# A list scheduler simulates the engines' timelines in its finer way: what becomes of the time?

## The chip, the cores and the metric

The kernel runs on one core of a Trainium2 chip. Its time is the device time of one execution in microseconds (us); TensorE, VectorE, ScalarE, GpSimd and SyncE (whose queue issues the DMA transfers) each run a list of instructions of their own, in order, and wait for each other by semaphores. In the profile they are PE (products), PEld (its weight loads), DVE, ACT, POOL and SP.

## The reference, cut to what matters

All in float32, 512 tokens of width 1024, two blocks of two layers each:

```python
def first_block(x, p, ...):                       # twice:
    z = rmsnorm(h) @ w_in + b_in                  # conv, pool, q, k, v, gates, index q and k
    ya = conv_module(...) * silu(c_gate)          # 31 taps, norm, product
    yb = pool_mixer(...) * silu(p_gate)
    yc = sparse_attention(q, k, v, qi, ki, wi) * silu(a_gate)   # top 128 keys of an index score
    h = h + concat([ya, yb, yc]) @ w_out
    h = h + (p[i] @ ple_w[i]) * sigmoid(h @ ple_gate_w[i])

def second_block(x, positions, meta_tokens, ...): # 16 meta tokens in front; twice:
    proj = h @ w_in[li]
    y_att = _mla(...)                             # latent attention, 4 heads
    y_rwkv, v_first = _rwkv_bidir(...)            # a recurrence, 8 heads, both directions
    h = layer_norm(a * h + concat([y_att, y_rwkv]) @ w_out[li])
    h = layer_norm(a * h + _hier_moe(h, ...))     # 32 experts, the best 2 of a token's group
```

## The kernel before, in words

The program is written with a tile framework: Python code calls one operation after another on tiles that come from pools with a fixed number of buffers, and nothing in it says when an operation runs. When the context that wraps the whole program closes, the framework's scheduler makes the list of each engine. It walks along a simulated timeline. Whenever an engine can take its next operation, it gets, of the operations that count as ready at that simulated moment (inputs done, a buffer free for the output), the one with the best priority. The priority is the order in which the Python code called them; a stretch of code can raise its own. So the simulated timeline does not appear in the result as times, only as an order: of instructions on each of the four compute engines, of transfers on SP's queue, and of who gets a buffer that comes free. On the chip each engine then runs its list strictly in order.

Stages, in the order of the program:

- `first_block` (lines 818 to 840), with `first_layer` (387 to 740) twice. Weights arrive in chunks of 256 columns (`raw`, line 291) and are split in two rounded parts, one on ScalarE (line 300), the rest on GpSimd (line 301), so that a float32 product becomes three fast ones (`mm3`, line 307). The layer's start turns normed rows (line 315) and rotates the index projections (lines 370 to 375). In the attention each unit (`terms`, lines 625 to 647, `values`, 649 to 664) makes logits (633), their maxima (636), a scaling of two columns (638), exponentials (640), a diagonal (646), turned terms (657) that VectorE or ScalarE evicts (275, 277), and values (662). Beside them the code lays six taps of the convolution (line 518, VectorE) and a share of dense projections.
- Between the blocks: norms and transposes by way of DRAM (lines 742 to 803).
- `mixers` (1258 to 1322), for each of the second block's layers: projections (1006), latent attention (1073 to 1209), and the recurrence in four pairs of heads (`rwkv_pair`, 1339 to 1726). A pair's last stage is a chain of nine steps: a product with the state (1636, added at 1638), the triangular inverse (1662, evicted at 1671), the update's product (1674, added on VectorE at 1677, two instructions a step). Its priority is raised by 300 places. Fill (projections, attention) is laid between the steps at a rate, `RATE`, that the source fixes.
- `out_rest` (1778 to 1857) and `moe` (1872 to 2086): output projection, norm, routing, then 16 pairs of experts, whose weights (100 MB a layer) stream through buffers of the pools (2227, 2231), and the norm at the end of the layer.

The lines that set priority and rate:

```python
            n += self.RATE[l]
            while fill is not None and (n > 0 or all(x == "end" for x in state)):
                ...
                c = next(fill, "end")
...
            with self.tc.high_priority(offset=self.AHEAD):      # AHEAD = 300
...
    with tile.TileContext(nc) as tc:                            # line 2328
        program(tc, A, out)
```

`lnexp2` (lines 975 to 983) makes a power of -1/2 on ScalarE by a logarithm (980) and an exponential (982).

Of the kernel before, what the change touches and what calls it, by code (L numbers as in the profile page):

```python
# [16 lines left out]
DRAM = bass.MemoryType.DRAM  # L17
# [10 lines left out]
# ---------------------------------------------------------------- constants of the shapes  # L28
def shape_constants():
    c = {}  # L30
    i = np.arange(128)
    c["ident"] = np.eye(128, dtype=np.float32)
    # lhsT of the swap x -> (-x2, x1) within each 64 rows
# [15 lines left out]
    # one over the pools' counts: of the first 16 tokens, of the later ones  # L49
# [13 lines left out]
def slot_codes():  # L63
    """per token tile and choice: the token, and its row among the choices' results"""
    v = np.zeros((128, 5, 2, 2), np.int32)
    for t, (t0, n) in enumerate(TT):
        tok = t0 + np.arange(n)
        for k in range(2):
            v[:n, t, k, 0] = tok
            v[:n, t, k, 1] = tok * 2 + k  # L70
    return v.reshape(128, 20)


def shape_constants2():
    """the second block's"""
# [9 lines left out]
    # masks of the chunk products: rows (slot, j), columns (kkd i | rd i); the b rows sit in slot q, and only they have  # L85
    # removal products there
# [10 lines left out]
    # masks of the doubling steps from blocks of 8 on, lower for T forward; the last belongs to the transposed  # L97
# [7 lines left out]
    # row j of each block of 8 on all of its partitions; a block's own columns; its unit rows, forward and backward  # L105
# [12 lines left out]
    # per choice and token tile: the token, and its row among the choices' results, less a number that no row has  # L118
# [14 lines left out]
# those of the recurrence stay only beside the mixers  # L133
# [6 lines left out]
# columns of the first block's projection  # L140
# [4 lines left out]
# per-partition parameter columns of a first-block layer  # L145
# [9 lines left out]
def cols(v):  # L155
    """[n*128] -> [128, n]"""
    return np.ascontiguousarray(v.reshape(-1, 128).T)
# [11 lines left out]
def pack_p2(x, l):  # L169
# [9 lines left out]
    for k in "gb":  # L179
        put("n1" + k, x[f"ln1_{k}_2"][l])  # L180
        # those of the norm before the layer
        put("n" + k, x[f"ln2_{k}_2"][l - 1] if l else x[f"emb_ln_{k}_2"])
# [18 lines left out]
class K:  # L201
# [26 lines left out]
    # frequently used tags  # L228
# [13 lines left out]
    def c(self, name, width=None):  # L242
        """a constant, or width columns from its first on"""
# [18 lines left out]
    # out[128, n] = in ** -0.5  # L262
# [3 lines left out]
    def load_cols(self, w, c0, n, kt=8):  # L266
        """rows (k p) of w, n columns from c0 -> [128, kt, n]"""
# [11 lines left out]
    # ------------------------------------------------------------ the first block  # L279
    # A float32 product in three passes of float32r: each operand is the sum of a rounded part and the rest, and only  # L280
    # the product of the two rests, below float32's last place, stays out.
# [6 lines left out]
    def raw(self, w, c0, n, kt):  # L288
        """kt*128 rows of w, n columns from c0"""
# [4 lines left out]
    def split_cols(self, w, c0, n):  # L294
        """n columns of w from c0 in two parts, [128, 8, n] each"""
# [8 lines left out]
    def mm3(self, ps, a, b, start, stop):  # L304
        """ps += a^T b, of their parts"""
# [3 lines left out]
    def columns(self, x, src, t):  # L309
        """a token tile's rows, turned, into its columns of x [128, 8, 512], in two parts"""  # L310
# [11 lines left out]
    def start_layer(self, l):  # L322
        """its small parameters, and its first weights"""
# [13 lines left out]
    def tile_rms(self, t, h, junk=None):  # L337
        """1/rms of a token tile's rows"""
# [7 lines left out]
    def tile_normed(self, x, t, h):  # L346
        """normed, and into its columns of x"""
# [4 lines left out]
    def zT(self, w, c, nT, m=128):  # L352
        """psum [m, 512] of columns c..c+m of the loaded chunk"""
# [5 lines left out]
    def go_on(self, topk=0):  # L359
        """what was left until the tensor engine had more to do; and some steps of the masks"""  # L360
# [17 lines left out]
    def silu_gate(self, ps, bias, hbias):  # L378
        """(tanh(z/2) + 1) * z : twice silu(z)"""
# [7 lines left out]
    def first_layer(self, l, h):  # L387
# [9 lines left out]
        # ---- index projections  # L397
# [27 lines left out]
        # ---- scores and the mask of the top 128  # L425
# [31 lines left out]
        # ---- queries, keys, values  # L457
# [25 lines left out]
        # ---- convolution: its input  # L483
# [20 lines left out]
        # ---- beside the attention: the taps, and dense work that yields its share of the tensor engine's time  # L504
# [3 lines left out]
        def conv_taps():  # L508
            # ---- the convolution
            for j in range(2):  # L510
# [3 lines left out]
                # u holds twice the gated value: the taps are halved  # L514
# [7 lines left out]
        def dense():  # L522
            # ---- the attention's gate
# [12 lines left out]
            # ---- pool mixer  # L536
# [31 lines left out]
            for j in range(2):  # L568
# [5 lines left out]
                # (psum + b) * scale, the gate to come  # L574
# [6 lines left out]
            # ---- the convolution's norm and product  # L581
# [30 lines left out]
            for j in range(2):  # L612
# [3 lines left out]
                # cs and the gate each hold twice their value: psum/2 + b, then the gate's half  # L616
# [7 lines left out]
        # ---- attention  # L624
        def terms(t, hp):
            """the softmax' terms of a tile of queries and two heads, and their sums' reciprocals"""
# [22 lines left out]
        def values(t, hp, pt, dgs):  # L649
# [3 lines left out]
            for i in range(2):  # L653
                # turned over and divided by the sum
# [29 lines left out]
        # ---- out projection and residual  # L684
# [15 lines left out]
        # ---- per-layer embedding, gated  # L700
# [39 lines left out]
    # ------------------------------------------------------------ between the blocks: the first one's result, normed, behind  # L740
    # the meta tokens; normed again: transposed and by rows, these without the gains and the biases, in DRAM
# [12 lines left out]
    def embedded(self, t, h):  # L754
        """the statistics of token tile t"""
# [21 lines left out]
        else:  # L777
            # the second norm of h*fg / r, with r*r = mean(h*h) + 1e-6: that of h*fg with r*r times its epsilon
# [30 lines left out]
    def lnexp(self, ps, scale, eps, n):  # L809
        """(ps*scale + eps) ** -0.5 of a psum tile, on the scalar engine"""  # L810
# [29 lines left out]
    # ------------------------------------------------------------ the second block  # L840
# [10 lines left out]
    def gy(self, dt=F32):  # L851
        """half of the transposed hidden state, or two of the mixers' outputs"""
        return self.g_tile("gy", [128, 2, L2], 4, dt)
# [5 lines left out]
    def wide(self):  # L859
        """1024 columns of the same store"""  # L860
# [5 lines left out]
    def rows2(self, *srcs):  # L866
        """[1024] rows of DRAM on every partition"""
# [5 lines left out]
    def stats(self, q, x, n, st, eps=1e-5):  # L873
        """the mean of x's rows, negated, and 1/deviation, of the rows' sums in st's first two columns"""
# [11 lines left out]
    def staged(tiles, *stages, between=iter(())):  # L886
        """for each tile its stages, those of later tiles before"""
# [6 lines left out]
    def scaled(self, out, q, n, g, b, fast=False):  # L894
        """out = q*g + b"""
# [7 lines left out]
    def hT_tiles(self):  # L903
        """the transposed hidden state in two parts, four [128, 2, 528] each"""
        return [(self.gy(F32R), self.big(F32R)[:, :2 * L2].rearrange("p (j t) -> p j t", j=2)) for _ in range(4)]

    def parts(self, hi, lo, x, eng=None):
        """x's rounded part, and the rest"""
# [3 lines left out]
    def angles(self):  # L912
        """cos and sin of the positions, [128 (four times 32 dims), 528], to DRAM"""
# [27 lines left out]
    def turned(self, q, t):  # L941
        """a normed token tile, transposed, in two psums"""
# [9 lines left out]
    def transposed2(self, hT, t, q):  # L952
        """those, times the gains and with the biases, in two parts"""
# [12 lines left out]
    def halves(self, lhs, rhs, m=128, start=True, stop=True, ps=None):  # L966
        """psums [m, 264] x 2 of sum_k lhs[k]^T rhs[k]"""
# [7 lines left out]
    def lnexp2(self, ps, scale, eps, out=None):  # L975
        """(ps*scale + eps) ** -0.5 of a pair of psums -> [128, 528]"""
# [12 lines left out]
    # 128 columns each of the projection: 0-1 queries, 2 keys and values, 3 the rotated keys (twice), 4-15 r, k, v, 16-18 low  # L989
    def proj_weights(self, l, i, eng=None):  # L990
        """in two parts"""
# [8 lines left out]
    def proj_tile(self, w, hT):  # L1000
        """psums [128, 264] x 2, of the parts"""
# [11 lines left out]
    def both(self, out, ps):  # L1013
        """out = the two psums"""
# [3 lines left out]
    def shifted(self, i, w, hT):  # L1018
        """the i-th tile of the recurrence's inputs; r, k and v go to DRAM"""
# [11 lines left out]
    def fill(self, l, hT, hs, yd, tiles):  # L1031
        """dense work beside the recurrence: its other inputs, the attention; yields its share of the tensor engine's time"""
# [19 lines left out]
    def rope2(self, z, o, cos, sin):  # L1052
        """o may be z"""
# [1278 lines left out]
```

## Time and profile before

| | us |
|---|---|
| median of the runs (two: 2854.81 and 2856.70) | 2855.76 |
| span of the profiled execution | 2857.8 |
| TensorE busy in it | 2472.6 |
| VectorE, ScalarE, GpSimd busy | 1496.6, 855.6, 822.8 |

The span runs from the first to the last instruction of one profiled execution, which lies 2.0 us above the median of the runs. Busy time counts overlapping instructions once. The granted clock is TensorE's, as a share of its full 2.4 GHz; its other level is 1.2 GHz. An idle time in front of an instruction is put down to what ended it.

### The profile page before, as it was taken

The numbers are of one execution on the slowest core, as the hardware profiler recorded it, in microseconds if no ns is written. First come the engines' busy times: TensorE is split into PE (matmuls) and PEld (weight loads), VectorE is DVE, ScalarE is ACT, GpSimd is POOL, SyncE is SP. The second block draws the span as 40 slices with busy tenths as digits, with TensorE's granted clock in tenths as the row PEclk, the third lists the DMA queues.
The fourth block names the chain that finished last, engine by engine and source line by source line (L and its number), as shares of the span: only waits on it lengthen the run. The fifth ranks groups of instructions, "written<-read, shape, count | busy, mean of one in ns | idle before, by whom it ended". The sixth has DMA issues, their size and how long they took to land. (4 is left out here: it accounts for less than half of the span.)

```text
span 2857.8 us, 48911 instructions
## 1 busy us (share of the span) xinstructions
PE 2472.6 (87%) x19771; PEld 1901.9 (67%) x19771; DVE 1496.6 (52%) x3308; ACT 855.6 (30%) x1698; POOL 822.8 (29%) x795
## 2 busy tenths in 40 slices
PE   7989997988996889999996889959888899969893
PEld 5766795766896777766765556549766667755552
DVE  3956234866245685566536321166866675362213
ACT  3233323233333433434402010133434344021111
POOL 5444424545421541222012100034523120120102
PEclk9999998999997989999998899979999999989997
DMA  5220122221126322101326899873220113279996
GB/s 158 60 78 30 50 82 63 63 70 38 61 64 192 108 92 85 34 29 51 124 68 217 269 369 365 280 218 118 84 89 15 44 51 120 82 261 367 371 364 234
DMA packets 312294, 394.16 MB, mean 138 GB/s; under 512 B 23683, under 2 KB 258819, under 8 KB 311809
## 3 DMA queue, kind: packets, MB, share of 16 engines
q1 hardware_dynamic: 304288, 376.70, 40.1%
q0 software_dynamic: 7776, 14.30, 1.4%
q8 instruction: 157, 2.57, 0.4%
q14 instruction: 73, 0.59, 0.1%
HBM read 352.02 MB, written 52.94 MB: 142 GB/s over the span
## 5 line engine op out<-in xcount | busy, mean ns | idle before, releaser
L301 POOL TENSOR_TENSOR wl<-raw,wh 128x1024 fp32r<-128x1024 f32 (+1 forms) x92 | 217.9, 2380 | 251.7 <-ACT wh L300 251.7
L1006 PE MATMUL sc<-gy,w 128*128 128x264 f32 x1216 | 223.9, 300 | 28.9 <-DVE ph L1864 11.3
L1006 PEld LDWEIGHTS sc<-gy,w 128*128 128x128 f32 x1216 | 183.0, 198 | 38.5 <-issue 13.3
L307 PE MATMUL ps<-wh,xh 128*128 128x256 f32 x640 | 190.6, 298 | 9.5 <-DVE a L374 9.5
L307 PE MATMUL ps<-wl,xh 128*128 128x256 f32 x640 | 184.2, 288 | 0.0
L307 PE MATMUL ps<-wh,xl 128*128 128x256 f32 x640 | 183.6, 287 | 0.0
L307 PE MATMUL ps<-xh,wh 128*128 128x512 f32 (+1 forms) x400 | 172.0, 430 | 0.0
L300 ACT ACTIVATE wh<-raw 128x1024 fp32r<-128x1024 f32 (+1 forms) x92 | 93.0, 1025 | 258.9 <-PE ps L307 154.7
L307 PE MATMUL ps<-xl,wh 128*128 128x512 f32 (+1 forms) x400 | 166.3, 416 | 0.1
L307 PE MATMUL ps<-xh,wl 128*128 128x512 f32 (+1 forms) x400 | 165.5, 414 | 0.0
L2023 POOL DMA_INDIRECT zd<-my,idx x32 | 31.6, 986 | 424.9 <-ACT my L277 424.9
L2241 PE MATMUL ps<-big,hTr 128*64 128x256 f32 x1168 | 153.9, 381 | 0.0
L1006 PE MATMUL sc<-big,w 128*128 128x264 f32 x608 | 134.1, 295 | 2.4 <-DVE big L910 2.4
L307 PEld LDWEIGHTS ps<-wh,xh 128*128 128x128 f32 x640 | 124.4, 194 | 14.0 <-DVE a L374 12.4
L307 PEld LDWEIGHTS ps<-wl,xh 128*128 128x128 f32 x640 | 124.6, 195 | 0.7
L307 PEld LDWEIGHTS ps<-wh,xl 128*128 128x128 f32 x640 | 124.6, 195 | 0.0
L2241 PEld LDWEIGHTS ps<-big,hTr 128*64 128x64 f32 x1168 | 93.1, 137 | 40.7 <-issue 2.8
L2188 DVE SCALAR_TENSOR_TENSOR mh<-mh,ps 128x256 f32<-128x256 f32 x32 | 13.5, 421 | 188.2 <-ACT mh L2187 188.2
L1006 PEld LDWEIGHTS sc<-big,w 128*128 128x128 f32 x608 | 101.1, 198 | 3.9 <-DVE big L910 3.5
L518 DVE SCALAR_TENSOR_TENSOR a<-pz,ph,a 128x512 f32<-128x512 f32 x120 | 102.0, 850 | 2.7
L1591 ACT ACTIVATE z<-ps,mix 128x512 f32<-128x512 f32 x144 | 76.8, 577 | 77.8 <-PE ps L1481 77.6
L1996 PEld LDWEIGHTS ps<-gy,big 128*128 128x128 f32 (+1 forms) x720 | 86.7, 190 | 18.8 <-issue 6.5
(500 smaller groups left out, 6037.8 us busy)
## 6 DMA issues: line engine op xcount, KB each, us to landing
big<-in_moe_w_dram SPq DMA_DIRECT2D x216, 512.0 KB, 9.2
w8m<-in_moe_w_dram SPq DMA_DIRECT2D x48, 1024.0 KB, 12.5
w<-in_moe_w_dram SPq DMA_DIRECT2D x36, 1024.0 KB, 12.3
raw<-in_w_in_dram SPq DMA_DIRECT2D x56, 512.0 KB, 3.6
big<-in_w_in_dram SPq DMA_DIRECT2D x36, 512.0 KB, 5.7
raw<-in_w_out_dram SPq DMA_DIRECT2D x16, 512.0 KB, 3.5
raw<-in_ple_gate_w_dram SPq DMA_DIRECT2D x16, 512.0 KB, 3.5
big<-zd SPq DMA_DIRECT2D x16, 512.0 KB, 8.1
```

What stands on the lines that cost most here:

```text
L300: nc.scalar.activation(hi[:, x:x + 4], v, AF.Copy)
L301: nc.gpsimd.tensor_tensor(lo[:, x:x + 4], v, hi[:, x:x + 4].bitcast(F32), op=ALU.subtract)
L307: self.nc.tensor.matmul(ps, a[x], b[y], start=start and j == 0, stop=stop and j == 2)
L518: nc.vector.scalar_tensor_tensor(acc, u[:, s:s + S], ph[:, tp + s:tp + s + 1], acc, op0=ALU.mult, op1=ALU.add)
L1006: self.nc.tensor.matmul(ps[x][:, :HALF], w[a][:, k], hT[k // 2][b][:, k % 2, x * HALF:(x + 1) * HALF], start=k == 0 and a == b == 0, stop= ...
L1591: nc.scalar.activation(Z[g][q][:, :self.WIDTH[g]], ps[:, :self.WIDTH[g]], AF.Copy, scale=self.c("half")[:, q:q + 1])
L1996: nc.tensor.matmul(ps[:, k * 128:(k + 1) * 128], h[t][:n, (4 * g + k) * 128:(4 * g + k + 1) * 128], sel[:n, t], start=t == tiles[0], stop= ...
L2023: ins = nc.gpsimd.indirect_dma_start(out=zd[:, :], out_offset=bass.IndirectOffsetOnAxis(ap=idx[:, j, 1:2], axis=0), in_=y, in_offset=None, ...
L2188: nc.vector.scalar_tensor_tensor(a, a, 1.0, p1[:, :256], op0=ALU.add, op1=ALU.mult)
L2241: nc.tensor.matmul(ps[q * 64:q * 64 + 64, :256], xT[:, k, q * 64:q * 64 + 64], w[q][k], start=k == 0, stop=k == 7)
```

## The change

The scheduler's simulated timeline comes from the framework's other, finer machine model. The program that is traced is the same: no operation, tile, pool, number of buffers, priority or rate is touched. The same diff empties comments and docstrings, leaving blank lines in their place, so line numbers stay as they are.

```diff
-    with tile.TileContext(nc) as tc:
+    with tile.TileContext(nc, schedule_with_timeline_sim=True) as tc:
         program(tc, A, out)
```

## Rows read from the trace of the kernel before

**Rows 1.** The page's first part: busy time, share of the span, instructions.

```profile
span 2857.8 us, 48911 instructions
PE 2472.6 (87%) x19771; PEld 1901.9 (67%) x19771; DVE 1496.6 (52%) x3308; ACT 855.6 (30%) x1698; POOL 822.8 (29%) x795
```

**Rows 2.** Busy time by stretches: start:end, length, engines, granted clock, DMA share, GB/s.

```profile
20.00:855.00 835.00, 761.65 (x4284) 608.72 (x4284) 462.05 (x929) 268.13 (x522) 376.39 (x281) 0.94 0.21 64
...
905.00:1555.00 650.00, 593.75 (x5853) 474.23 (x5851) 398.58 (x934) 233.63 (x472) 169.30 (x192) 0.94 0.27 88
...
1590.00:1860.00 270.00, 245.72 (x1748) 151.15 (x1744) 48.82 (x109) 29.62 (x61) 21.01 (x21) 1.00 0.97 335
...
1905.00:2530.00 625.00, 568.90 (x5747) 463.06 (x5745) 394.17 (x891) 230.55 (x455) 156.11 (x183) 0.96 0.28 90
...
2565.00:2815.00 250.00, 225.34 (x1679) 140.54 (x1677) 47.74 (x108) 29.62 (x61) 21.02 (x21) 1.00 1.05 363
```

**Rows 3.** TensorE's waits, 20 to 855: total us, times, longest.

```profile
PE po L662 <- DVE attT L275: 21.5, 10, 3.9
PE ps L315 <- DVE b L349: 14.2, 5, 5.6
PE ps L436 <- DVE a L374: 9.9, 2, 4.9
PE ps L307 <- DVE a L374: 9.5, 2, 4.8
PE px L657 <- POOL diag L646: 6.8, 6, 1.9
PE po L662 <- ACT attT L277: 6.1, 4, 2.2
```

**Rows 4.** TensorE's waits, 905 to 1555: the longest group.

```profile
PE ps L1662 <- DVE rr L1638: 5.7, 5, 1.8
```

**Rows 5.** TensorE's waits, 1905 to 2530: the longest group.

```profile
PE ps L971 <- ACT u L1708: 6.5, 3, 2.7
```

**Rows 6.** The timeline, 198 to 216: start, us, instruction, idle before and releaser.

```profile
202.66 5.14 POOL L301 TENSOR_TENSOR wl<-raw,wh 128x1024 fp32r<-128x1024 f32 x2 [2.70 <-ACT wh L300]
...
203.03 2.57 DVE L518 SCALAR_TENSOR_TENSOR a<-pz,ph,a 128x512 f32<-128x512 f32 x1
...
205.53 2.30 DVE L638 TENSOR_SCALAR sm<-sm 128x2 f32<-128x2 f32 x1
...
208.90 1.09 PE L662 MATMUL po<-attT,a 128*64 128x128 f32 x4 [3.87 <-DVE attT L275]
...
209.91 0.80 PE L307 MATMUL ps<-xl,wh 128*128 128x512 f32 x1
```

**Rows 7.** Instructions of lines 518 and 638: count, ns min/median/max.

```profile
L518 DVE SCALAR_TENSOR_TENSOR a<-pz,ph,a x120: 731/752/2896, 172.7 to 677.3; 128x512 f32<-128x512 f32 x120
L638 DVE TENSOR_SCALAR sm<-sm x32: 155/169/2397, 165.7 to 728.5; 128x2 f32<-128x2 f32 x32
```

**Rows 8.** VectorE's timeline: updates of line 1677, 1154 to 1176 and 1236 to 1249.

```profile
1163.73 0.58 DVE L1677 TENSOR_TENSOR hr<-hr,ps 64x128 f32<-64x128 f32 x2
1174.14 0.58 DVE L1677 TENSOR_TENSOR hr<-hr,ps 64x128 f32<-64x128 f32 x2
...
1240.80 0.59 DVE L1677 TENSOR_TENSOR hr<-hr,ps 64x128 f32<-64x128 f32 x2 [2.14 <-PE ps L1674]
...
1244.32 0.59 DVE L1677 TENSOR_TENSOR hr<-hr,ps 64x128 f32<-64x128 f32 x2 [0.52 <-issue]
```

**Rows 9.** Instructions of line 1677: count, ns min/median/max, first and last start.

```profile
L1677 DVE TENSOR_TENSOR hr<-hr,ps x128: 240/286/293, 1134.2 to 2489.8; 64x128 f32<-64x128 f32 x128
```

**Rows 10.** Groups by line, VectorE: count, busy us, mean ns, idle before.

```profile
L518 DVE SCALAR_TENSOR_TENSOR a<-pz,ph,a 128x512 f32<-128x512 f32 x120 | 102.0, 850 | 2.7
...
L638 DVE TENSOR_SCALAR sm<-sm 128x2 f32<-128x2 f32 x32 | 23.9, 746 | 0.4
```

**Rows 11.** Groups by line, ScalarE: the table loads.

```profile
L980 ACT ACT_TABLE_LOAD x28 | 35.9, 1283 | 0.5
...
L982 ACT ACT_TABLE_LOAD x25 | 32.1, 1283 | 0.4
```

## The prediction

> **What bounds the kernel now.** I read the page's first part first: TensorE is busy for 2472.6 us of a span of 2857.8 us, VectorE for half of it, ScalarE and GpSimd for under a third [rows 1]. So 385.2 us of the span has no product in flight, and an order of instructions can win no more than that and what the clock gives. Where it lies comes from busy time by stretches [rows 2]: in the three long stretches of dense work (the first block 20 to 855, the two layers of mixers 905 to 1555 and 1905 to 2530) TensorE is busy for 761.65, 593.75 and 568.90 us, so it is idle for 73.4 + 56.3 + 56.1 = 185.8 us. In the two expert stretches the DMA share is 0.97 and 1.05, and TensorE is idle for 24.3 + 24.7 = 49 us: there the weights' arrival sets the pace, and no order of compute changes the bytes. The remaining 385.2 - 185.8 - 49 = 150.4 us is start, routing, norms between layers and the tail: short stretches in which each operation needs the one before it.
>
> So the change can act on 185.8 us of idle time, and on the clock beside it: the granted clock was 0.94, 0.94 and 0.96 in the three stretches [rows 2], against 1.00 in the expert stretches. With levels of 1.2 and 2.4 GHz, a shortfall of 0.06 is half speed for 12% of the time, worth at most 0.06 x 835 + 0.06 x 650 + 0.04 x 625 = 114 us if TensorE had work all through it.
>
> Then I read who ended TensorE's waits. In the first block six groups make up nearly all: 34.4 us behind the attention's evictions and diagonals (21.5 + 6.1 + 6.8) and 33.6 us at the starts of the layers (14.2 + 9.9 + 9.5) [rows 3]. In the mixers the waits are scattered: the longest group of each layer is 5.7 and 6.5 us [rows 4, 5]. One of the attention's waits shows what an order can do [rows 6]: at 203.03 a convolution tap on VectorE took 2.57 us and at 205.53 a two-column scaling took 2.30 us, both while GpSimd was in its 5.14 us of weight splitting; the eviction behind them came late, and TensorE stood idle for 3.87 us before line 662, although the next thing in its queue was more products of line 307 of a group it had already begun. Those could have gone first. The list has line 662 in front, as it would if on the simulated timeline its input was there by then.
>
> **The change part by part.** No operation, tile, pool or buffer count changes; what changes is the simulated time at which an operation counts as ready, and so the order of the list that each engine gets, DMA issues on SP's queue included.
>
> *Gain in the attention.* The 34.4 us [rows 3] are waits of the kind just shown. The ends are 0 (the new list makes the same mistakes elsewhere) and 34.4. I take half, -17 us, because the example has ready work behind the wait and I have looked at one.
>
> *Gain in the mixers.* 112.4 us idle. Many small groups mean that no single dependency rules. The ends are 0 and half, 56; I take a quarter, -28 us, nearer to 0, because TensorE is already busy 91% here and much of what is left is the recurrence's own chain.
>
> *Starts of layers.* The 33.6 us [rows 3] are a norm, a transpose and a rotation in sequence. I take 0, with ends of -10 and +10.
>
> *Clock.* Of 185.8 us idle 45 would go, a quarter; half of a quarter of 114 us gives -14 us. Ends 0 and -28.
>
> *What is lost: the recurrence's steps.* The loop in mixers lays fill (projections, attention) between chain steps at a rate written in the source, and the chain has its priority raised by 300 places. The scheduler sees that priority only when it gives an engine its next operation. A chain interval, from one update at line 1677 to the next, was 3.52 us where the chain went first (1240.80 to 1244.32) and 10.41 us where other work lay between (1163.73 to 1174.14) [rows 8]. There are 128 instructions of that line [rows 9], two a step, so 64 steps. If one in ten goes from short to long, 6.4 x 6.9 = 44 us of chain; TensorE has other work beside most of it, so I charge half, +22 us. The ends are -20 (some long ones become short) and the first rival's +110.
>
> *What is lost or won by collisions.* Taps of line 518 took 752 ns in the median and up to 2896, the scaling of line 638 took 169 in the median and up to 2397 [rows 7]; the stretched ones lay beside GpSimd's splits [rows 6]. By the means [rows 10] that is (850 - 752) x 120 + (746 - 169) x 32 = 30 us of VectorE in the first block. A new order hits other operations. Ends -20 and +30, and I take +5 us, near 0, since VectorE is not the bound. The Trainium skill, page "SBUF — State Buffer", section "SBUF: two separate sides", says that VectorE and GpSimd share a port pair as an exclusive lock which whoever starts first keeps for its whole instruction. The rows agree, and the rule speaks against the change: a simulation of one engine's durations need not hold this lock. By it, if 20 of the first block's splits newly met a VectorE operation that TensorE waits for, each would cost up to 2.2 us, and the sum below would come out some 40 us higher.
>
> *ScalarE's table loads.* Lines 980 and 982 already make 28 and 25 loads of 1283 ns [rows 11], because logarithm and exponential alternate with other functions. A new order on ScalarE may change their number by a third either way: 18 x 1.28 = 23 us of an engine that is busy 30%. I charge +5, ends -10 and +23.
>
> *Experts, edges.* 0, ends -10 and +15: the DMA queue stays full in the expert stretches, and what might move is only how early the first loads are issued.
>
> Sum: -17 - 28 - 14 + 22 + 5 + 5 = -27 us on a span of 2857.8, so 2831 us. The median of the runs is 2 us below that span, so 2829. The ends of this case alone, since the terms won't all fall on one side, I put at 2790 and 2890.
>
> **The rivals.** *The lists are fixed further ahead, and the chain loses its place* (slower). A finer timeline can also have the engine's queue in it; then fill is handed to an engine while it is still busy, and the raised priority comes too late. For it: the long intervals [rows 8] show that this price exists already, and fill is ready nearly always where TensorE is 91% busy. Against it: the operations and priorities are the same. If three steps in four become long, 48 x 6.9 = 331 us of chain; if a third of this outlasts the fill, +110 us: 2966. It decides once the mean interval grows by 2.7 us (64 x 2.7 / 3 = 57 us). It would be seen in the mixers' windows, with TensorE's idle time there above 112 us.
>
> *The stalls go* (much faster). If the finer timeline fits the chip, half of the 185.8 us idle goes, and half of that share of the clock: -93 - 28, and with +20 of the losses -101: 2755. For it speaks the 3.87 us wait. Against it: waits that end on the chain of the recurrence and on layer starts stay whatever the order.
>
> *The lists hardly differ.* If readiness is mostly a matter of data and of buffers that come free, the order stays nearly what it was, and the time stays within 10 us of 2856. Against it: with 48911 instructions [rows 1] and hoisting wherever an engine is free, small differences in time spread.
>
> **How the numbers follow.** Forecast 0.44, chain loses its place 0.29, stalls go 0.17, hardly differs 0.10. A change of 2% (57 us: below 2799 or above 2913) is about what a measurement of this kernel can tell from none. Faster by more: most of the third case and a little of the first, 0.20. Slower by more: most of the second and a little of the first, 0.30. Within: 0.50. The range is cut where one in ten is left on each side: 2765 (the lower half of the third case) and 2975 (the upper third of the second).
>
> **What would show it.** The three dense stretches of the new profile against [rows 2]: the forecast wants their idle time at some 140 us in place of 186 and clocks of 0.95 to 0.97; waits at line 662 near 15 us; line 1677's intervals longer in the mean by under 1 us; expert stretches of the same length with a DMA share near 1; table loads between 40 and 75. Wrong would be the picture of the first rival: mixers lengthened, TensorE idle beside a chain that waits. Wrong in another way would be a change of the edges or the expert stretches, for which I have charged nothing: if the weights' loads were issued tens of us later, each us would show at the end.

## The result, and the profile after

The changed kernel takes 2895.05 us (two runs, 2894.33 and 2895.76) against 2855.76 before: 1.0131 of it, with a 95% interval of 1.0101 to 1.016. It is slower by 29 to 46 us, less than the 2% that I had called a change; the forecast was 2829.

I read the page's first part first.

```profile
span 2894.0 us, 48878 instructions
PE 2473.1 (85%) x19771; PEld 1914.5 (66%) x19771; DVE 1501.0 (52%) x3308; ACT 853.4 (29%) x1698; POOL 837.7 (29%) x795
```

TensorE's busy time is what it was [rows 1] and the span is 36 us longer, so in the sum the change is idle time. Then the stretches, cut near the events of [rows 2] (first block, mixers, experts, mixers, experts):

```profile
20.00:810.00 790.00, 735.11 (x4281) 592.77 (x4279) 463.42 (x931) 269.44 (x526) 379.84 (x282) 0.98 0.23 66
860.00:1545.00 685.00, 596.54 (x5780) 476.25 (x5779) 406.23 (x931) 231.60 (x468) 183.59 (x193) 0.91 0.26 85
1580.00:1850.00 270.00, 243.47 (x1720) 151.67 (x1720) 48.65 (x114) 29.36 (x61) 21.94 (x22) 1.00 0.96 334
1885.00:2570.00 685.00, 587.76 (x5771) 481.00 (x5772) 405.17 (x896) 231.22 (x460) 168.52 (x195) 0.91 0.28 90
2605.00:2850.00 245.00, 219.88 (x1638) 137.67 (x1634) 45.54 (x101) 28.05 (x59) 20.05 (x20) 1.00 1.06 367
```

Two opposite results stand in it. The first block is 45 us shorter: idle 54.9 us instead of 73.4, and the same products busy for 735.1 us instead of 761.7, since the granted clock is 0.98 instead of 0.94. The mixers are 35 and 60 us longer: idle 88.5 and 97.2 us instead of 56.3 and 56.1, at a clock of 0.91 instead of 0.94 and 0.96. The expert stretches are within 5 us. These stretches are round numbers and cut the mixers a little differently in the two kernels. Between two products that bound them (the first of line 1006 and the first of the routing) the mixers are 32 and 51 us longer, with 99.7 and 103.9 us idle instead of 77.4 and 69.1; the account at the end goes by these.

TensorE's waits in the first block, the groups that answer to the attention's in [rows 3]:

```profile
PE po L662 <- DVE attT L275: 7.6, 6, 2.1
PE px L657 <- POOL diag L646: 3.2, 4, 0.9
PE po L662 <- ACT attT L277: 1.1, 3, 0.4
```

34.4 us have become 11.9; with two new groups at line 662 of 2.5 and 2.4 us it is 16.8. In the mixers (860 to 1545, then 1885 to 2570) the longest groups were 5.7 and 6.5 us [rows 4, 5]. Now:

```profile
PE ps L971 <- ACT u L1708: 13.3, 2, 11.4
PE ps L971 <- DMA u<-side: 10.4, 2, 9.5
...
PE ps L971 <- ACT u L1708: 21.3, 3, 15.0
PE ps L971 <- DMA u<-side: 10.0, 1, 10.0
```

These four hold 55 us, 46 of them in four single waits, and all are ends of a pair of heads: line 1708 belongs to the group norm behind the chain, `side` is what a pair's output is multiplied with. The first is best read in VectorE's timeline at the end of the third pair, with SP's queue at the same time below it:

```profile
1384.32 0.69 DVE L1699 COPY u<-ps 128x512 f32<-128x512 f32 x1 [1.80 <-PE ps L1688]
1390.63 5.75 DVE L897 TENSOR_TENSOR big<-big,big 16x1024 f32<-16x1024 f32 x5 [5.62 <-DMA big<-in_emb_g_dram]
1396.31 0.69 DVE L1707 TENSOR_TENSOR u<-u,u 128x528 f32<-128x528 f32 x1
```

```profile
1383.06 0.33 SPq L1759 DMA_DIRECT2D big<-in_emb_g_dram  x1
...
1385.17 6.62 SPq L2227 DMA_DIRECT2D big<-in_moe_w_dram  x3
1391.84 1.85 SPq L1712 DMA_DIRECT2D u<-side  x1
```

Line 897 scales the residual rows for the last fill (`out_parts`, line 1767). VectorE's list has five of it in front of line 1707, and the first waits until 1390.63 for a gain that was issued at 1383.06. Line 1707's own input was there at 1386.70 (line 1706 on ScalarE, 1385.87 and 0.83 us), so it starts 9.6 us late, and TensorE waits 11.4 us for what follows from it. On SP's queue three expert loads of 512 KB stand in front of the side loads (264 KB each). Before, the order was the other one on both, VectorE's list first:

```profile
1417.56 0.71 DVE L1707 TENSOR_TENSOR u<-u,u 128x528 f32<-128x528 f32 x1 [1.53 <-ACT u L1706]
...
1428.43 1.20 DVE L897 TENSOR_TENSOR big<-big,big 16x1024 f32<-16x1024 f32 x1
```

```profile
1415.68 0.57 SPq L1712 DMA_DIRECT2D u<-side  x1
1416.30 0.42 SPq L1713 DMA_DIRECT2D u<-side  x1
...
1418.00 0.61 SPq L1759 DMA_DIRECT2D big<-in_emb_g_dram  x1
```

The other thing to see is the chain, in TensorE's timeline at the start of the fourth pair:

```profile
1407.75 6.40 PE L1767 MATMUL ps<-w,gy 128*16 128x256 f32 x20 [2.49 <-DVE u L1721]
1414.08 0.65 PE L1636 MATMUL ps<-hr,big 128*64 128x128 f32 x4
1414.66 1.90 PE L1767 MATMUL ps<-w,gy 128*16 128x256 f32 x8
1416.49 0.68 PE L1662 MATMUL ps<-rr,big 128*64 128x64 f32 x8
1417.10 4.92 PE L1767 MATMUL ps<-big,gy 128*16 128x256 f32 x22
1421.95 0.45 PE L1674 MATMUL ps<-w,big 128*64 128x64 f32 x8
```

In this pair 8 to 22 products of fill stand between two products of the chain wherever there are any. Before, there were mostly 2 to 8:

```profile
1433.93 1.04 PE L1767 MATMUL ps<-w,gy 128*16 128x256 f32 x4
1434.90 0.45 PE L1674 MATMUL ps<-w,big 128*64 128x64 f32 x8
```

But one interval of each layer's fourth pair before, of some 25 us, held 96 and 92 of them: the old list had long steps too, fewer of them. Over all eight pairs the interval from one update at line 1677 to the next (differences of starts in VectorE's timeline, 56 of them) rose from 6.03 to 7.51 us in the mean.

### The profile page after: what moved, and what is told of

It reads as the page before. It is cut to its first block, busy times and chain, and to the rows that moved or that the text cites. A ratio compares the mean times of both kernels' runs of the same rounds, so it can differ in the third digit from the quotient of the medians.

```text
span 2894.0 us, 48878 instructions
## 1 busy us (share of the span) xinstructions
PE 2473.1 (85%) x19771; PEld 1914.5 (66%) x19771; DVE 1501.0 (52%) x3308; ACT 853.4 (29%) x1698; POOL 837.7 (29%) x795
## 5 line engine op out<-in xcount | busy, mean ns | idle before, releaser
L1006 PE MATMUL sc<-gy,w 128*128 128x264 f32 x1216 | 232.5, 296 | 24.5 <-DVE ph L1864 11.4
L1006 PEld LDWEIGHTS sc<-gy,w 128*128 128x128 f32 x1216 | 192.5, 196 | 30.8 <-issue 13.5
L1006 PE MATMUL sc<-big,w 128*128 128x264 f32 x608 | 166.1, 295 | 1.1 <-DVE big L910 1.1
L518 DVE SCALAR_TENSOR_TENSOR a<-pz,ph,a 128x512 f32<-128x512 f32 x120 | 119.6, 996 | 1.9
L1006 PEld LDWEIGHTS sc<-big,w 128*128 128x128 f32 x608 | 113.8, 196 | 3.8 <-DVE big L910 1.8
L1634 POOL MEMSET rr<- 64x256 f32 x56 | 17.4, 311 | 292.5 <-PE ps L1662 265.2
```

Of the source, the lines that this page charges most:

```text
L518: nc.vector.scalar_tensor_tensor(acc, u[:, s:s + S], ph[:, tp + s:tp + s + 1], acc, op0=ALU.mult, op1=ALU.add)
L1006: self.nc.tensor.matmul(ps[x][:, :HALF], w[a][:, k], hT[k // 2][b][:, k % 2, x * HALF:(x + 1) * HALF], start=k == 0 and a == b == 0, stop= ...
L1634: nc.gpsimd.memset(r[64 - q * 64:128 - q * 64], 0.0)
```

## The experiments

All in us, each beside runs of the kernel before (2853 to 2859 in the median). "Finer" is the changed kernel, "coarser" the one before. Line numbers shift by a few where lines were added. Mixers: from the first product of line 1006 to the first of the routing (line 1947), layer 0 and layer 1, by the trace; 694 and 648 before, 725 and 699 in the changed kernel.

| run | median | ratio to before (95%) | mixers |
|---|---|---|---|
| border alone, coarser | 2856.5 | 0.9996 (0.9979 to 1.0013) | 692, 647 |
| finer in the first block alone | 2807.7 | 0.9824 (0.9804 to 0.9844) | 686, 645 |
| finer in the second block alone | 2933.7 | 1.0267 (1.0238 to 1.0296) | 731, 692 |
| finer, fill held behind steps | 2888.5 | 1.0108 (1.0079 to 1.0137) | 725, 693 |
| finer, priority 3000 | 2889.1 | one run | 722, 696 |
| coarser, priority 0 | 2917.1 | 1.0213 (1.0186 to 1.0239) | 719, 686 |
| finer, fill in half products | 2886.8 | 1.0114 (1.0092 to 1.0136) | 728, 687 |
| finer, last fill after the chain | 2889.1 | 1.0118 (1.0083 to 1.0153) | 728, 694 |
| finer, VectorE's order fixed | 2886.4 | 1.0117 (1.0098 to 1.0136) | 724, 692 |
| finer, side loads raised by 3000 | 2890.6 | 1.0123 (1.0102 to 1.0143) | 726, 699 |
| finer, the last two together | 2891.0 | 1.0132 (1.0109 to 1.0154) | 725, 692 |
| coarser, VectorE's order spoilt | 2879.4 | 1.0092 (1.0075 to 1.011) | 705, 658 |
| finer, VectorE's and SP's order fixed | 2861.4 | 1.0013 (1.0004 to 1.0023) | 711, 679 |
| finer, SP's order alone fixed | 2875.7 | 1.0062 (1.0042 to 1.0082) | 715, 690 |
| both orders, fill held | 2867.9 | 1.0032 (1.0018 to 1.0045) | 711, 692 |
| both orders, less fill laid | 2878.8 | 1.0062 (1.0041 to 1.0082) | 711, 699 |

### Which half

The theory: the finer timeline's lists serve the attention and harm the mixers, each by itself. The rival: the mixers only suffer from what a faster first block hands over. The scheduler can take a part of the program as a block of its own:

```diff
-        with ExitStack() as e1:
-            k.pool(e1, "b1", 3, 0)
-            k.first_block()
+        with tc.block(name="one"):              # second run: , schedule_with_timeline_sim=True
+            with ExitStack() as e1:
+                k.pool(e1, "b1", 3, 0)
+                k.first_block()
```

and the third run wraps everything after `first_block` in the same way, with the flag.

> The first block is made a block of its own for the scheduler, which still works by the coarser machine model: no finer timeline anywhere. This prices the border alone (nothing of the second block may be mixed in among the first block's instructions). Theory and rivals agree here: the border costs the prefetch of the second block's first weights, 0 to 30 us; 2856 to 2886 us, with the first block ending near 876 us and the mixers' stretches at 650 and 625 us as before.

> The same border, with the finer timeline for the first block alone. Theory (the finer lists help the attention, where queues of independent products stand behind an eviction, and hurt the mixers, where a chain must be let through): the first block ends some 46 us earlier than in the border's own run and the mixers are as long as before: 46 us below that run, 2810 to 2840 us. Rival (the mixers are slow because the faster first block hands them other buffers, transfers or leftovers): the mixers are long here too, some 80 us above the border's run less 46, 2890 to 2920 us.

> The other half: the second block is a block of its own and alone gets the finer timeline; the first block keeps the coarser one. Theory: mixers' stretches near 685 us each, intervals of the recurrence's update near 8 us in the mean, 80 to 90 us above the border's run: 2935 to 2970 us. Rival (it is what the first block hands over): the mixers stay at 650 and 625 us, 2856 to 2886 us.

The border costs nothing. With it the first block alone gains 49 us (2856.5 to 2807.7), and the second alone loses 77. In the second run the three dense stretches read

```profile
20.00:807.00 787.00, 731.07 (x4281) 590.10 (x4279) 460.67 (x931) 269.05 (x525) 379.34 (x282) 0.98 0.21 66
860.00:1500.00 640.00, 583.76 (x5814) 466.45 (x5813) 396.42 (x932) 232.85 (x470) 170.81 (x192) 0.95 0.28 89
1870.00:2470.00 600.00, 542.79 (x5586) 439.10 (x5585) 383.42 (x876) 226.01 (x447) 155.59 (x183) 0.96 0.27 87
```

that is, the first as in the changed kernel and the mixers at the clocks of before. The rival falls: the mixers are short behind a fast first block (686 and 645 us), and the third run's are long (731 and 692 us) behind the slow one. This second run is also the version that beats both kernels, by 1.6 to 2.0% against before.

### The chain's place

Here the theory was my first rival's: the chain stands behind fill that TensorE's list has in front of it.

```diff
-                c = next(fill, "end")
+                with self.tc.issue_after(self.gate) if self.gate is not None else ExitStack():
+                    c = next(fill, "end")
...
-                        nc.tensor.matmul(pH[hs, d * 64:d * 64 + 64], ...)
+                        self.gate = nc.tensor.matmul(pH[hs, d * 64:d * 64 + 64], ...).ins
```

> The changed kernel with one more rule: fill that the source lays behind a step of the recurrence may not stand in TensorE's list ahead of that step's last product (line 1674). No operation is added. Theory (products of later fill are put into TensorE's list while a step's input is not there yet, and the step then stands behind them): intervals of line 1677 in the third pair of heads fall from 15 us to 4 to 7 us, the 11 and 15 us gaps at the ends of the chains go because fill is left, the mixers come to 640 to 665 us each: 2825 to 2865 us. Rival (steps are long because of their own inputs, from VectorE and ScalarE, whose lists are also fixed further ahead): intervals stay above 8 us in the mean, and TensorE stands idle where the fill was: 2900 to 2960 us.

It gave some 7 us, which the intervals don't tell from none, with the mean interval at 7.45 us. (The expectation counts pairs from zero; its third is the fourth elsewhere in this text.) That pair's intervals were 15.8, 16.3, 13.3 and then 6.7. Neither side's picture came. As the source reads, it lays several parts of the last fill at once there, since its credit has run up while that fill was not allowed yet; no run tests this by itself. The edge holds fill behind the step before it, not behind the step after.

```diff
-    AHEAD = 300
+    AHEAD = 3000                                 # in the kernel before: AHEAD = 0
```

> The changed kernel with the recurrence raised by 3000 places instead of 300. Theory (the priority is only seen when TensorE is handed its next product, and by then products of fill stand ahead in its list): nothing changes, 2885 to 2905 us, intervals of line 1677 as in the changed kernel (8.85 us in the mean in the second pair, 11.2 in the fourth). Rival (the finer timeline only changes which operations compete, and 300 places no longer reach past them): intervals come back to 4 to 7 us, 2830 to 2860 us.

> The kernel before, with the recurrence raised by 0 places: the chain loses its place by hand, under the coarser timeline. If the chain's place is what the changed kernel lost, mixers without it should look like those of the changed kernel: intervals of line 1677 of 7 to 11 us in the mean in all pairs, mixers 30 to 50 us longer each, 2910 to 2960 us. Rival (the priority was worth little before, so its loss can't be the cause): within 15 us of the kernel before, 2840 to 2870 us.

A priority ten times higher changes nothing: the second pair's mean interval is 8.84 us and the fourth's 11.24, as without it, and TensorE's list differs in 30 of some 6950 rows (neighbouring products of one line and the same tiles as one row). So the distance is not what is lacking. In the kernel before, that priority is worth 63 us (2917.1 against 2854.0), with a mean interval of 8.23 us. All of it is in the mixers, 26 and 38 us, with 4.6 and 5.1 us idle between the third and fourth chains (4.7 and 3.6 before). A place in the list that the priority gives is thus worth much under the coarser timeline, and the finer one has some of it no longer.

```diff
-                for k in range(7):
-                    nc.tensor.matmul(ps[:n, :256], ..., wo[c][k], ...)
+                for x in range(2):
+                    for k in range(7):
+                        nc.tensor.matmul(ps[:n, x * 128:x * 128 + 128], ..., wo[c][k][:, x * 128:x * 128 + 128], ...)
```

> The changed kernel, with each product of line 1767 (the fill beside the last pair's chain) as two of 128 columns: the same columns, twice as many instructions, each half as long. In the changed kernel 20 to 22 rows of that line, 4.4 to 5.9 us, lie between two products of the chain. If what is put ahead is a number of instructions: again some 20 rows, now 2.5 to 3.5 us, and the last pair's intervals fall from 14 to 16 us to 9 to 11 us. If it is a time (the finer timeline takes the chain's input to come that late): some 40 rows, the intervals stay at 14 to 16 us. The time in both cases 2860 to 2910 us.

TensorE's timeline of that run:

```profile
1429.35 0.68 PE L1662 MATMUL ps<-rr,big 128*64 128x64 f32 x8
1429.96 2.94 PE L1768 MATMUL ps<-w,gy 128*128 128x128 f32 x24
1432.83 0.45 PE L1674 MATMUL ps<-w,big 128*64 128x64 f32 x8
1433.21 2.72 PE L1768 MATMUL ps<-w,gy 128*128 128x128 f32 x22
```

22 to 24 products again, now 2.7 to 2.9 us instead of 4.9, and intervals of 9.6 to 12.4 us, with one of 15.5, instead of 14.6 to 16.3: what is put ahead is a number of instructions. But the chain of the last pair took some 79 us in both, because the same fill now lies beside all seven intervals instead of the first five, and the time is the same within 9 us.

```diff
-        while self.state[:3] != ["end"] * 3 or self.state[3] not in ("chain", "end"):
+        while self.state != ["end"] * 4:
```

> The changed kernel, with the fill of line 1767 laid only behind the last pair's chain (in the changed kernel it begins with the chain). Nothing then can stand ahead of this chain but the attention's end. Theory (the chain waits behind fill, and the fill is gone when the pair's end needs cover): the fourth pair's intervals fall from 11.2 and 10.0 us to 4 to 6 us, its chain ends some 40 us earlier, the waits of 9.5 to 15 us at lines 971 go, and the products of 1767 follow in its place; 20 to 40 us gained in two layers, 2855 to 2875 us. Rival (the chain is long by its own steps on VectorE and ScalarE): intervals stay above 8 us, and the fill comes on top: 2930 to 2990 us.

This run turned me from the chain to the ends. The fourth pair's chain in VectorE's timeline, the changed kernel and this run:

```profile
L1677 DVE TENSOR_TENSOR hr<-hr,ps x16: 270/286/292, 1407.9 to 1486.9; 64x128 f32<-64x128 f32 x16
```

```profile
L1677 DVE TENSOR_TENSOR hr<-hr,ps x16: 269/286/292, 1410.0 to 1438.0; 64x128 f32<-64x128 f32 x16
```

The chain ends 49 us earlier, its mean interval is 4.0 us, and over all pairs it is 5.90 us, shorter than before the change. The time is the same within 6 us, and so are the mixers: the fill follows behind instead of beside. In these last pairs long intervals cost nothing that the run can tell, since fill in front of the chain is work done. It says nothing of the second pairs, whose chains stay at 67 and 65 us (62 and 63 in the changed kernel, 43 and 33 before). What stayed in this run are the waits at the ends; the longest of TensorE's from 1405 to 1470 is

```profile
PE ps L971 <- DMA u<-side: 8.7, 1, 8.7
```

### The ends of the pairs

The edits: line 897 on VectorE held behind the third pair's last operation; the two side loads raised; both. The fourth run puts the defect into the kernel before.

```diff
+        if i == 2:
+            self.third = last                    # line 1721's second instruction
...
-            self.scaled(h, h, n, g, b)
+            with self.tc.issue_after(self.third):
+                self.scaled(h, h, n, g, b)
```

```diff
+        with self.tc.high_priority(offset=3000):
             bonus, gate = self.u()[:, :L2], self.u()[:, :L2]
             nc.sync.dma_start(bonus, self.side[i])
             nc.sync.dma_start(gate, self.side[4])
```

```diff
+            self.third = sub                     # line 1707 of the third pair
...
+            if t == tiles[-1]:                   # first: this tile's line 897 on VectorE
+                self.tc.add_manual_dep(self.third, first.name, ...)
```

> The changed kernel with one order fixed on VectorE: the scaling of the residual rows (line 897, called at the start of the last fill) may not stand ahead of the third pair's last operation (line 1721). Between the third and the fourth chain the changed kernel has TensorE idle for 16.7 and 18.2 us (before 4.7 and 3.6), since line 1707 stands in VectorE's list behind four or five operations of line 897 that wait for a DMA. Theory (this order is the greater part of the loss): idle there falls to 4 to 7 us, the half-speed stretch behind it goes, 24 to 34 us gained, 2861 to 2871 us. Rival (the fill is gone by then, so TensorE is idle there whatever VectorE's order): idle stays above 12 us each, 2885 to 2900 us.

> The changed kernel, with the two loads that a pair's end needs (lines 1712 and 1713) raised by 3000 places, so that on SP's queue they go ahead of eight expert loads of 512 KB. In the changed kernel TensorE waits 9.5 and 10.0 us for them behind the last pair. Theory: these two waits go, 12 to 20 us gained with the clock behind them, 2875 to 2883 us. Rival (the end of the pair is then held up by its own operations, and the expert stretch starts no earlier because the weights' loads set it): under 5 us, 2888 to 2896 us.

> Both orders of the two runs before in the changed kernel. Theory (two separate places): the gains add, 36 to 54 us, 2841 to 2859 us, that is, at the kernel before; what is left of the mixers' loss is then some 30 to 40 us in the chains of the second pairs and the clock. Rival (one place's gain is eaten by the other): no better than the better of the two, 2861 to 2875 us.

> The kernel before, coarser timeline, with the defect put in by hand: line 1707 of the third pair may not stand ahead of the last residual tile's line 897 on VectorE. Theory: TensorE's idle time between the third and fourth chains rises from 4.7 and 3.6 us to 14 to 20 us, and the time by 20 to 34 us, 2876 to 2890 us. Rival (under the coarser timeline fill is left to cover it): under 8 us, 2855 to 2864 us.

The defect put into the kernel before costs 26 us, in the middle of what was expected. TensorE's waits of that run, in the first layer's mixers and then the second's, where line 1708 has become 1710:

```profile
PE ps L971 <- ACT u L1710: 18.6, 2, 16.7
...
PE ps L971 <- ACT u L1710: 23.9, 3, 19.2
```

The repair in the changed kernel gave some 4 us by the ratios (1.0131 to 1.0117), which the intervals don't tell from none, and the raised loads did nothing. TensorE's waits of the repaired kernel, in the first layer's mixers and then the second's:

```profile
PE ps L971 <- DMA u<-side: 19.1, 2, 9.7
...
PE ps L971 <- DMA u<-side: 19.8, 2, 10.7
```

Line 1707 now runs at 1390.51, right behind its input, but line 971 then waits at the same place for the side loads. They were issued at 1394.96, behind three expert loads. Raising their priority moved them nowhere: in that run's queue they still come right after the three and, in the first layer's last pair, after eight and one. So I held the expert loads, by their order alone:

```diff
+        self.sides[i] = nc.sync.dma_start(gate, self.side[4]).ins
...
     def load_w(self, src, kt):
+        self.loads += 1
+        with self.tc.issue_after(self.sides[2 if self.loads <= 3 else 3]):
+            return self.load_one(src, kt)
```

> The changed kernel with two orders fixed: on VectorE line 897 not ahead of the third pair's end (as in the run that gained nothing alone), and on SP's queue the expert loads not ahead of the side loads of the third pair (the first six) and of the fourth (the others). In the run with VectorE's order alone TensorE waited 9.7 and 10.7 us for the side loads at the very place where it had waited for line 1707. Theory (two lists hold up the same end, and each hides the other): idle between the third and fourth chains falls from 16.7 and 18.2 us to 4 to 8, that behind the fourth chain from 26.4 and 28.5 to 17 to 22; 30 to 55 us gained, 2840 to 2865 us. Rival (the fill is gone at the ends of pairs, so something else is late next): above 2880 us.

> The same with SP's queue alone held, VectorE's list as the changed kernel has it. Theory: the waits behind the fourth chain go, those between the third and fourth stay (line 1707 still behind line 897), 8 to 20 us gained, 2875 to 2887 us. Rival (the side loads are late because their buffers come free late or the DMA engines are full, not because of their place in the queue): waits of 8 to 10 us stay, 2888 to 2896 us.

SP's order alone gains some 20 us (1.0131 to 1.0062), both together 34 (to 1.0013): on top of SP's, VectorE's order is worth 14 us, although alone it gained 4. The mixers' two layers are 14 and 20 us shorter than in the changed kernel, which is all of it. The stretch from the third chain's last update to the fourth's first, by layer (columns as in [rows 2]; TensorE's idle time is the length less the first busy figure), before, changed, and with both orders fixed:

```profile
1408.10:1427.50 19.40, 14.67 (x227) 11.53 (x223) 6.17 (x14) 9.86 (x18) 0.62 (x2) 0.78 0.83 286
2410.80:2427.00 16.20, 12.58 (x175) 9.53 (x169) 6.17 (x13) 8.60 (x16) 0.31 (x1) 0.76 0.81 293
```

```profile
1381.00:1407.90 26.90, 10.23 (x84) 7.03 (x82) 13.32 (x14) 6.70 (x12) 16.14 (x6) 0.63 0.68 235
2424.50:2452.60 28.10, 9.90 (x84) 6.94 (x83) 15.43 (x13) 6.69 (x12) 12.61 (x5) 0.64 0.78 243
```

```profile
1382.60:1405.60 23.00, 12.71 (x94) 7.85 (x93) 10.22 (x14) 6.58 (x12) 4.66 (x2) 0.70 0.82 275
2403.80:2422.50 18.70, 10.71 (x83) 7.19 (x80) 3.80 (x8) 6.69 (x12) 0.31 (x1) 0.62 0.94 306
```

Idle 4.7 and 3.6 us, then 16.7 and 18.2, then 10.3 and 8.0. The 8 to 10 us waits for side loads behind the last pair are gone as well: the stretch from the fourth chain's end to the routing has 19.3 and 21.1 us idle instead of 26.4 and 28.5 (21.7 and 17.1 before). Between the third and fourth chains a wait for a side load stays in each layer, of 6.5 and 4.2 us, although it is now issued ahead of the expert loads (1386.79 in the first); in front of it lie the residual rows, the gain, the shift and a weight, and this speaks for the rival's full DMA engines at this one place.

That side loads wait for what stands before them (the first layer's took 9.8 us from issue to landing) agrees with the Trainium skill, page "DMA: Bandwidth & Descriptors", section "Queues, rings and completion order": on each DMA engine the descriptors of a ring are consumed in ring order.

### What is left

> The kernel with both orders fixed (2861 us), and the fill held behind the steps of the recurrence as in the fourth run. Some 49 us of the mixers' loss are left there (711 and 679 us against 694 and 648). Theory (the rest is fill spent too early, in front of the chain): holding it shortens the intervals and leaves fill for the ends, 10 to 30 us gained, 2831 to 2851 us. Rival (the source's own rate decides when the fill is gone, and the chains' place costs little): within 8 us of 2861.

> The kernel with both orders fixed, with the rate at which the source lays fill beside the recurrence cut from 3.2 and 2.6 to 2.9 and 2.35. Theory (fill runs out before the third pair's end): more is left there, idle between the third and fourth chains falls from 10.3 and 8.0 us to 4 to 6, 5 to 15 us gained, 2846 to 2856 us. Rival (the lists take fill in the order of readiness, whatever the source's rate): within 5 us of 2861; or slower, 2866 to 2880, where the early pairs then go short.

Neither found it. With the fill held, the time is 2867.9, on the rival's side; with less fill laid it is slower, as the rival's second branch says. There the idle time between the chains went only from 10.3 and 8.0 to 8.6 and 6.5 us. So in the mixers some 49 us (711 + 679 against 694 + 648) stay without a cause that a run shows. By the trace 31 us of it is idle time spread over chains and gaps in parts of at most 6 us, and the rest is TensorE busy for longer at a lower clock.

One candidate is left untested, the chain's place outside the last pairs. With both orders fixed the mean interval is still 7.47 us, the second pairs' chains are 18 and 30 us longer than before the change (the stretch behind them is 18 and 19 us shorter), and no run under the finer timeline shortened those. Priority 0 in the kernel before lengthened the mean interval by 2.20 us and the mixers by 63; in proportion, 1.44 us would make some 41 of the 49. That is an estimate from these two runs and shows nothing by itself.

## Why the prediction was wrong

The sign was missed in the mixers. Their -28 counted the waits of the old list that could go and had no term for waits that a new list makes; the place for one was "*Experts, edges.* 0 ...: what might move is only how early the first loads are issued." How early they are issued was the point, not for the experts but for the two side loads that then stand behind them. The same step passed over the other head of a list, line 897 on VectorE. I had named SP's queue as something that the change reorders and priced nothing on it. Fixing these two orders takes 34 us off: nearly all that the change cost in sum (37), but only two fifths of what the mixers lost (32 + 51 = 83). The cause of the other 49 us stays open, and the first rival's price may be part of it.

Point by point:

- *Attention.* Half of 34.4 us was to go, with waits at line 662 near 15 us. They are 13.6 (7.6 + 2.5 + 2.4 + 1.1), and the block's idle time fell by 18.5. Right in size; that the first block's own lists do it is shown by the run with the finer timeline there alone, that ready products now go first is not.
- *Clock.* Charged -14 for all three stretches. In the first block alone the same products were busy 26.5 us less; between the two events that bound the mixers TensorE was busy 9 and 16 us longer, at a lower clock, which gives as much back. The term was mis-sized, and it goes where the idle time goes.
- *Mixers.* -28 was the wrong sign: idle 185.7 us in place of 112.4 by the stretches, 57 us more between the bounding products. "Many small groups mean that no single dependency rules" was true of the list before and says nothing of the next one: the new list made four waits of 9.5 to 15 us where the longest single wait in the same stretches had been 4.4.
- *The recurrence's steps.* Lengthened by 1.48 us in the mean, where I had under 1: 83 us over 56 intervals (the 64 updates have 7 intervals in each of 8 pairs), against 44 us, half of it charged. In the last pairs this costs nothing that a run can tell: the chain 49 us shorter, the time the same within 6. What it costs in the other pairs stays open; the kernel before with priority 0 paid half of its lengthening (63 of 123 us), the share that I had charged.
- *The first rival.* Its mechanism is there (fill put ahead by number of instructions, priority without effect), and its picture too (idle above 112 us), but not its price: the interval stayed under the 2.7 us at which I let it decide, and 34 us of the loss were elsewhere.
- *Lists hardly differ.* Out: the time moved by 39 us where it wanted at most 10, and TensorE's two lists, of 6760 and 6956 rows taken as above, differ in 1836 rows.
- *Collisions, table loads, starts.* Line 518 now takes 996 ns in the mean instead of 850, while the first block got faster; the exclusive lock in the Trainium skill, page "SBUF — State Buffer", section "SBUF: two separate sides", agrees with such stretched taps (18 took over 1.2 us instead of 6, each of them beside an instruction of GpSimd), and the 40 us that I had put beside it did not come. The starts' three groups came to 20.2 us (11.7 + 8.5) in place of 33.6, a little beyond the -10 at which I had ended them. The table loads stayed at 28 and 25 [rows 11], where I had +5.

```profile
L518 DVE SCALAR_TENSOR_TENSOR a<-pz,ph,a 128x512 f32<-128x512 f32 x120 | 119.6, 996 | 1.9
L638 DVE TENSOR_SCALAR sm<-sm 128x2 f32<-128x2 f32 x32 | 17.7, 553 | 0.4
```

The halves by themselves make about -50 and +76 us, 26 in sum, and the whole +37 (29 to 46). With intervals of some 6 and 8 us on the halves, the runs don't show that the difference is one.

## What to carry to other kernels

When a scheduler's model changes, judge it by stage: here the same switch was worth -49 us in one block and +77 in the other, and using it where it helps took one line. Before pricing a new order, look for the short operation or the load that a latency-bound end needs, and ask what bulk work of the same list can come to stand in front of it, on every list, DMA queues included. Where two lists hold up the same end, repairing one may show nothing (VectorE's alone gained 4 us, on top of SP's 14): read what the wait has become before you drop the cause.

## What the runs showed that I had not expected

- In the last pairs the chain's steps could be three times as long (14.6 to 16.3 us instead of 3.6 to 4.8) at no cost that a run can tell, as TensorE worked through them. Five scalings that waited 5.6 us for a load and then took 5.75 cost 11.4 us of TensorE.
- The granted clock fell in such a gap and stayed low behind it: in the changed kernel it was 0.57 over the gap, then 0.50, the 1.2 GHz level, for 12 us in which TensorE was busy again for 8.19 (the stretch of the 11.4 us wait and the two behind it, columns as above).

```profile
1386.00:1398.00 12.00, 0.55 (x3) 0.27 (x2) 6.37 (x6) 1.60 (x4) 5.93 (x1) 0.57 0.99 340
1398.00:1410.00 12.00, 8.19 (x34) 4.60 (x35) 7.08 (x7) 4.24 (x6) 11.35 (x5) 0.50 0.25 89
1410.00:1440.00 30.00, 30.00 (x168) 18.90 (x167) 5.89 (x16) 0.76 (x2) 0.61 (x2) 0.97 0.09 28
```
